# A transformer block's attention by head pairs in double PSUM banks, with rotated queries and keys transposed behind half a projection

## The chip, the cores and the metric

The kernel runs on one core of a Trainium2 chip. The metric is the device time of one execution in microseconds, as the median of several runs. The engines named below are TensorE (PE, the matmuls), VectorE (DVE), ScalarE (ACT), GpSimd (POOL) and SyncE (SP, which issues the DMAs). Each takes its instructions in the order of its own list and waits where an operand isn't ready.

## The reference

The program computes two transformer blocks in fp32, for one sequence of 256 tokens and width 1024. The change touches only the first block's mixer:

```python
h = rms_norm(x, norm1_g)
u_a, v_a, q, k, v = split(h @ w_in, ...)            # five parts of 512 columns
a_out = spatial_gating(gelu(u_a), gelu(v_a), ...)    # 8 groups, chunks of 128 tokens
q, k = apply_rope(q, cos, sin), apply_rope(k, cos, sin)   # 8 heads of 64
b_out = dilated_attention(q, k, v)                   # three banded branches, weighted by their denominators
mix = concat(rms_norm(a_out), rms_norm(b_out))
x = x + mix @ w_out
x = x + peer(rms_norm(x, norm2_g), ...)              # router and experts
```

Behind it come the experts and a second block of two hybrid layers, which the change doesn't touch.

## The kernel before, in words

Matmuls are made from two halves of each operand: a number is split into a high half (rounded by ACT, L98) and a low half (the rest, by DVE, L99), and three matmuls (`mm3`, L116 to L118) make one product. Weights come in units of 512 KB (`fetch`, L88) into a ring of four `raw` buffers; a buffer is free for the next load when its low half has been made. In the first block the units are used in this order: four for `v_a`, four each for q, k and v (`project`, matmuls of 128x512), four for the gate `u_a` (`gate_u`, matmuls of 128x256, 24 to a unit), eight for `w_out`, and then those of the router.

The order of the instructions on each engine isn't that of the source: a scheduler lays out the lists from the source's order, the dependencies and the buffers of the pools. Pools in PSUM are `ps_b` (four single banks, tag `pp`) and `ps_m` (three single banks, tag `mm`, and one for `po`). These steps matter here:

- x is transposed four blocks at a time (L234); ACT scales and rounds each (L238) and DVE makes the low half.
- `rotated` (L290 to L307) turns q or k by the rope tables: DVE multiplies and adds (L296 to L302), PE transposes the sum (L306), ACT copies it out (L307).
- `attend(hp)` makes the scores of a pair of heads (L342), each head in a bank of its own. DVE adds the mask and reduces to the maximum (L349) and negates it (L351), ACT takes the exponential and its sum (L353), DVE takes the reciprocal (L355) and scales (L357).
- `gather_v(hp)` transposes the probabilities, one head to a bank (L369), DVE copies them out (L371), and PE multiplies by v (L373) into `po`. `mixed` (L284 to L288) makes the high half, the low half and the square of the result.
- `spatial(k)` does the spatial gating's matmuls (L385) and DVE adds the bias (L387).
- `finish_half` (L274 to L281) sums squares for a norm by matmuls with a column of ones (L278); `norm_rows` (L219 to L226) normalizes a block of rows and transposes it in two halves (`transposes`, L163 to L167).

The attention and the gating are written in this order:

```python
attend(0); pps = project(2); ...
attend(1); gather_v(0); attend(2); gather_v(1); attend(3); gather_v(2); gather_v(3)
for k in range(4):
    spatial(k)
    gate_u(k)
```

Of the kernel before, what the change touches and what calls it, by code (L numbers as in the profile page):

```python
# [9 lines left out]
F32 = mybir.dt.float32  # L10
# [6 lines left out]
ALU = mybir.AluOpType  # L17
# [8 lines left out]
T = 256  # L26
# [12 lines left out]
def kernel(  # L39
# [47 lines left out]
    def load(dst, src):  # L87
        nc.sync.dma_start(out=dst, in_=src)  # L88
# [109 lines left out]
    with ExitStack() as c1:  # L198
# [4 lines left out]
        ps_b = c1.enter_context(tc.tile_pool(name="ps_b", bufs=4, space=PSUM, side="right"))  # L203
        ps_m = c1.enter_context(tc.tile_pool(name="ps_m", bufs=3, space=PSUM))

# [61 lines left out]

        def project(chunk):
            pps = [ps_b.tile([128, 512], F32, name="pp") for _ in range(2)]
            x_stationary(pps, xh, xl, [w_in_n[chunk * 4 + i] for i in range(4)])  # L270
            return pps

        def finish_half(base, name):
            ps = ps_m.tile([128, 2], F32, name="mm")  # L274
            for k in range(1, 4):
# [13 lines left out]

        def rotated(pps, dst):  # L290
            for tb in range(2):
                a = w1.tile([128, 8, 2, 32], F32, name="ra")
                b = w1.tile([128, 8, 2, 32], F32, name="rb")
                p4 = pps[tb].rearrange("p (h c j) -> p h c j", h=8, c=2)
# [7 lines left out]
                V.tensor_tensor(out=a, in0=a, in1=b, op=ALU.add)  # L302
                pt = ps_m.tile([128, 4, 128], F32, name="mm")
                af = a.rearrange("p h c j -> p (h c j)")
                for j in range(4):
                    P.transpose(out=pt[:, j, :], in_=af[:, j * 128:(j + 1) * 128], identity=id_t)  # L306
                S.activation(out=dst[:, :, tb * 128:(tb + 1) * 128], in_=pt, func=AF.Copy)  # L307
# [17 lines left out]

        pr = ps_m.tile([128, 2, 128], F32, name="mm")
        for tb in range(2):
# [9 lines left out]
        def attend(hp):  # L337
            pss = [ps_m.tile([128, 2, T], F32, name="mm") for _ in range(2)]
            for tb in range(2):
                for e in range(2):  # L340
                    s = slice(64 * e, 64 * e + 64)
                    P.matmul(out=pss[e][:, tb, :], lhsT=qT[s, hp, tb * 128:(tb + 1) * 128], rhs=kT[s, hp, :],  # L342
                             start=True, stop=True)
            for e in range(2):
                sm = w1.tile([128, 2, T], F32, name="sm", bufs=4)
                mx = w1.tile([128, 2], F32, name="mx", bufs=4)
                ls = w1.tile([128, 2], F32, name="ls", bufs=4)
                for tb in range(2):
                    V.tensor_tensor_reduce(out=sm[:, tb, :], in0=pss[e][:, tb, :], in1=mask_t[:, tb, :], scale=0.125,  # L349
                                           scalar=GONE, op0=ALU.add, op1=ALU.max, accum_out=mx[:, tb:tb + 1])  # L350
                V.tensor_scalar(out=mx, in0=mx, scalar1=-1.0, scalar2=None, op0=ALU.mult)  # L351
                for tb in range(2):
                    S.activation(out=sm[:, tb, :], in_=sm[:, tb, :], func=AF.Exp, bias=mx[:, tb:tb + 1],  # L353
                                 accum_out=ls[:, tb:tb + 1])
                V.reciprocal(out=ls, in_=ls)  # L355
                for tb in range(2):
                    V.tensor_scalar(out=sm[:, tb, :], in0=sm[:, tb, :], scalar1=ls[:, tb:tb + 1], scalar2=None,  # L357
                                    op0=ALU.mult)
                probs[2 * hp + e] = sm

        def gather_v(hp):
            po = ps_m.tile([128, T], F32, name="po", bufs=1)
            for e in range(2):
                h = 2 * hp + e
                sm = probs[h]
                pt = ps_b.tile([128, 512], F32, name="pp").rearrange("p (a b t) -> p a b t", a=2, b=2)
                for tb in range(2):
                    for sb in range(2):
                        P.transpose(out=pt[:, sb, tb, :], in_=sm[:, tb, sb * 128:(sb + 1) * 128], identity=id_t)  # L369
                pT = w1.tile([128, 2, T], F32, name="pT")  # L370
                V.tensor_copy(out=pT, in_=pt.rearrange("p a b t -> p a (b t)"))  # L371
                for sb in range(2):
                    P.matmul(out=po[64 * e:64 * e + 64, :], lhsT=vr[:, sb, h * 64:(h + 1) * 64], rhs=pT[:, sb, :],  # L373
                             start=(sb == 0), stop=(sb == 1))
            mixed(4 + hp, po)
# [4 lines left out]
        def spatial(k):  # L380
            pg = ps_m.tile([128, 2, 128], F32, name="mm")
            for e in range(2):
# [12 lines left out]
        attend(0)  # L395
        pps = project(2)
        for tb in range(2):
            S.activation(out=vr[:, tb, :], in_=pps[tb], func=AF.Copy, scale=rx[tb])
        load(ws_t, w_s)
# [647 lines left out]
```

## Time and profile before

| | before |
|---|---|
| median of 3 runs | 1279.85 us (1278.71 to 1280.3) |
| profiled execution | 1281.43 us, of which the span is 1279.3 us |
| busy in the span | PE 97%, DVE 76%, ACT 50%, POOL 1% |
| granted TensorE clock | mean 0.996 of full speed |
| v's projection ends, attention begins | 62.9 us |
| last weighted sum of the attention ends | 82.1 us |
| gate's projections end | 93.2 us |

The times of the trace count from the start of the span. Busy shares are over the whole span; the part that the change touches lies in its first 122 us. A row of a timeline gives the start and the length of an instruction, or of several in a row (x4), its engine, line and tiles, and in brackets the idle time before it with what ended it. Most matmuls of fp32 operands that aren't split show as two records.

### The profile page before, as it was taken

The numbers are of one execution on the slowest core, as the hardware profiler recorded it, in microseconds if no ns is written. First come the engines' busy times: TensorE is split into PE (matmuls) and PEld (weight loads), VectorE is DVE, ScalarE is ACT, GpSimd is POOL, SyncE is SP. The second block draws the span as 40 slices with busy tenths as digits, with TensorE's granted clock in tenths as the row PEclk, the third lists the DMA queues.
The fourth block names the chain that finished last, engine by engine and source line by source line (L and its number), as shares of the span: only waits on it lengthen the run. The fifth ranks groups of instructions, "written<-read, shape, count | busy, mean of one in ns | idle before, by whom it ended". The sixth has DMA issues, their size and how long they took to land.

```text
span 1279.3 us, 22833 instructions
## 1 busy us (share of the span) xinstructions
PE 1247.1 (97%) x8952; PEld 1108.9 (87%) x8952; DVE 975.2 (76%) x1907; ACT 641.4 (50%) x1031; POOL 14.8 (1%) x27
## 2 busy tenths in 40 slices
PE   7999999999999999999999999999999999999997
PEld 5777998999999999998888888788878998789995
DVE  6877899944466999998999997655566766768565
ACT  7556544444454443344444445544445566354661
POOL 0001000000000000000000000000000000000000
PEclk9999999999999999999999999999999999999999
DMA  7723555565555445455555556855555634355420
GB/s 258 258 82 127 165 164 167 174 199 186 182 188 169 161 163 166 165 163 184 178 172 179 180 171 235 287 194 191 188 168 176 192 125 132 110 206 191 139 83 33
DMA packets 61819, 219.10 MB, mean 171 GB/s; under 512 B 7064, under 2 KB 8496, under 8 KB 61584
## 3 DMA queue, kind: packets, MB, share of 16 engines
q1 hardware_dynamic: 60272, 213.03, 50.4%
q0 software_dynamic: 1440, 4.62, 1.2%
q8 instruction: 70, 1.15, 0.4%
q14 instruction: 37, 0.30, 0.1%
HBM read 214.33 MB, written 3.16 MB: 170 GB/s over the span
## 4 chain that ended last, share of the span: by engine, by line
PE 85%; DVE 8%; ACT 4%; DMA 2%; issue 1%; SPq 0%; DVEq 0%; ACTq 0%
PE pu L116 9%; PE pv L116 9%; PE pu L118 9%; PE pu L117 9%; PE pv L118 9%; PE pv L117 9%; PE pp L118 7%; PE pp L117 7%; PE pp L116 7%; DVE ulo L99 3%; PE pg L656 1%; PE pg L657 1%; ACT uhi L98 1%; PE mm L795 1%; PE rt_ps L116 1%
## 5 line engine op out<-in xcount | busy, mean ns | idle before, releaser
L99 DVE TENSOR_TENSOR ulo<-raw,uhi 128x1024 fp32r<-128x1024 f32 x390 | 474.9, 1221 | 164.7 <-ACT uhi L98 164.2
L98 ACT ACTIVATE uhi<-raw 128x1024 fp32r<-128x1024 f32 x390 | 411.3, 1056 | 338.4 <-PE pu L117 205.2
L116 PE MATMUL pu<-xh,uhi 128*128 128x256 f32 x1024 | 293.8, 287 | 2.2 <-ACT ga L462 2.2
L118 PE MATMUL pu<-xh,ulo 128*128 128x256 f32 x1024 | 292.5, 286 | 1.6 <-DVE ulo L99 1.5
L117 PE MATMUL pu<-xl,uhi 128*128 128x256 f32 x1024 | 290.8, 284 | 0.0
L116 PE MATMUL pv<-uhi,wh 128*128 128x512 f32 x512 | 203.9, 398 | 0.4 <-ACT wh L98 0.4
L118 PE MATMUL pv<-uhi,wl 128*128 128x512 f32 x512 | 200.9, 392 | 0.6 <-DVE wl L99 0.6
L117 PE MATMUL pv<-ulo,wh 128*128 128x512 f32 x512 | 200.5, 392 | 0.0
L116 PEld LDWEIGHTS pu<-xh,uhi 128*128 128x128 f32 x1024 | 196.8, 192 | 3.9 <-ACT ga L462 3.1
L118 PEld LDWEIGHTS pu<-xh,ulo 128*128 128x128 f32 x1024 | 196.9, 192 | 3.4 <-DVE ulo L99 2.6
L117 PEld LDWEIGHTS pu<-xl,uhi 128*128 128x128 f32 x1024 | 196.9, 192 | 0.0
L116 PE MATMUL pp<-xh,uhi 128*128 128x256 f32 x496 | 141.4, 285 | 0.0
L118 PE MATMUL pp<-xh,ulo 128*128 128x256 f32 x496 | 141.0, 284 | 0.0
L117 PE MATMUL pp<-xl,uhi 128*128 128x256 f32 x496 | 140.6, 284 | 0.0
L98 ACT ACTIVATE wh<-ga 128x256 fp32r<-128x256 f32 x128 | 53.0, 417 | 173.9 <-PE pv L117 171.9
L118 PEld LDWEIGHTS pv<-uhi,wl 128*128 128x128 f32 x512 | 96.1, 188 | 22.9 <-DVE wl L99 1.2
L116 PEld LDWEIGHTS pv<-uhi,wh 128*128 128x128 f32 x512 | 96.2, 188 | 20.6 <-ACT wh L98 0.8
L117 PEld LDWEIGHTS pv<-ulo,wh 128*128 128x128 f32 x512 | 96.3, 188 | 20.0
L118 PEld LDWEIGHTS pp<-xh,ulo 128*128 128x128 f32 x496 | 94.1, 190 | 1.1 <-issue 1.0
L116 PEld LDWEIGHTS pp<-xh,uhi 128*128 128x128 f32 x496 | 94.2, 190 | 0.9 <-issue 0.7
L117 PEld LDWEIGHTS pp<-xl,uhi 128*128 128x128 f32 x496 | 94.1, 190 | 0.6 <-issue 0.4
L659 DVE SCALAR_TENSOR_TENSOR ga<-pg,ga 128x288 f32<-128x288 f32 (+1 forms) x96 | 87.2, 939 | 7.3 <-PE pg L657 7.3
(271 smaller groups left out, 1643.9 us busy)
## 6 DMA issues: line engine op xcount, KB each, us to landing
raw<-in_expert_u_dram SPq DMA_DIRECT2D x128, 512.0 KB, 3.4
raw<-in_expert_v_dram SPq DMA_DIRECT2D x128, 512.0 KB, 3.3
raw<-in_w_t_dram SPq DMA_DIRECT2D x58, 512.0 KB, 3.6
raw<-in_w_out_dram SPq DMA_DIRECT2D x24, 512.0 KB, 3.4
raw<-in_w_in_n_dram SPq DMA_DIRECT2D x16, 512.0 KB, 5.5
raw<-in_w_n_dram SPq DMA_DIRECT2D x16, 512.0 KB, 3.3
raw<-in_w_query_dram SPq DMA_DIRECT2D x12, 512.0 KB, 3.8
raw<-in_w_in_t_dram SPq DMA_DIRECT2D x4, 512.0 KB, 4.5
```

Of the source, the lines that this page charges most:

```text
L98: S.activation(out=hi, in_=src, func=AF.Copy)
L99: eng.tensor_tensor(out=lo, in0=src, in1=hi.bitcast(F32), op=ALU.subtract)
L116: P.matmul(out=ps, lhsT=lh, rhs=rh, start=start, stop=False)
L117: P.matmul(out=ps, lhsT=lh, rhs=rl, start=False, stop=False)
L118: return P.matmul(out=ps, lhsT=ll, rhs=rh, start=False, stop=stop).ins
L656: P.matmul(out=pg[:, t - lo_t, :], lhsT=o1[:, q, :, l], rhs=oh[:, q, :, l], start=True, stop=False)
L657: P.matmul(out=pg[:, t - lo_t, :], lhsT=o1[:, q, :, l], rhs=ol[:, q, :, l], start=False, stop=True)
L659: V.scalar_tensor_tensor(out=gv, in0=pg, scalar=1.0 / 32768.0, in1=gv, op0=ALU.mult, op1=ALU.mult)
L795: P.matmul(out=po[64 * e:64 * e + 64, tb, :], lhsT=v[:, sb, h * 64:(h + 1) * 64], rhs=w[:, e, n * 128:(n + 1) * 128], start=(sb == 0), sto ...
```

## The change

It does five things.

- `ps_m` becomes two double banks (`banks(n)`, tags `mm0` and `mm1`, one buffer each); all else takes a single bank of `ps_b` (`one_bank()`). The transposes of x and those of `norm_rows` put both halves of a row block into one double bank.
- `project` works by halves of two units. q's rotated transposes stand behind the first half of k's projection, k's behind the first half of v's; the rotation works in a tile that shares its buffers with the transposed probabilities.
- `attend` puts both heads of a pair into the double bank `mm0`: four reductions, one negation, four exponentials, one reciprocal and four scalings.
- `gather_v` puts the eight transposes of a pair into the double bank `mm1`, copies them out in one instruction, and runs the sums by v with both heads side by side.
- The mask is loaded ahead of the gain `g_v`.

```diff
...
-        ps_m = c1.enter_context(tc.tile_pool(name="ps_m", bufs=3, space=PSUM))
+        ps_m = c1.enter_context(tc.tile_pool(name="ps_m", bufs=1, space=PSUM))
+        def banks(n):
+            return ps_m.tile([128, 2, 512], F32, name="mm", tag=f"mm{n % 2}")
+        def one_bank():
+            return ps_b.tile([128, 512], F32, name="pp")
...
             r = rms_scale([src[:, 0:512], src[:, 512:1024]], scr)
+            bk = banks(tb)
...
-                transposes(ps_pool, xn, xh, xl, tb, 4 * n, 4)
+                transposes(ps_pool, xn, xh, xl, tb, 4 * n, 4, bk[:, n, :])
...
         for tb in range(2):
+            bk = banks(tb)
             for q in range(0, KD, 4):
-                pt = ps_m.tile([128, 4, 128], F32, name="mm")
+                pt = bk[:, q // 4, :].rearrange("p (j t) -> p j t", j=4)
...
-        def project(chunk):
-            pps = [ps_b.tile([128, 512], F32, name="pp") for _ in range(2)]
-            x_stationary(pps, xh, xl, [w_in_n[chunk * 4 + i] for i in range(4)])
-            return pps
+        def project(chunk, pps, half):
+            x_units([(pps + [0, 6], w_in_n[chunk * 4 + c], 2 * c) for c in range(2 * half, 2 * half + 2)], xh, xl)
...
-        rotated(project(0), qT)
+        ppq, ppk = [[one_bank() for _ in range(2)] for _ in range(2)]
+        project(0, ppq, 0)
+        project(0, ppq, 1)
+        rot = rotated(ppq)
+        project(1, ppk, 0)
+        transposed(rot, qT)
+        project(1, ppk, 1)
+        load(mask_t, att_mask.rearrange("(b p) s -> p b s", p=128))
+        rot = rotated(ppk)
+        ppv = [one_bank() for _ in range(2)]
+        project(2, ppv, 0)
+        transposed(rot, kT)
         bcast(g_v.rearrange("p a b -> p (a b)"), gains[0, 1024:2048], load)
-        rotated(project(1), kT)
-        load(mask_t, att_mask.rearrange("(b p) s -> p b s", p=128))
...
         def attend(hp):
-            pss = [ps_m.tile([128, 2, T], F32, name="mm") for _ in range(2)]
+            pss = banks(0)
...
+            each = [(e, tb, slice(tb * T, (tb + 1) * T), slice(2 * e + tb, 2 * e + tb + 1))
+                    for e in range(2) for tb in range(2)]
+            for e, tb, c, n in each:
+                V.tensor_tensor_reduce(out=sm[:, e, c], in0=pss[:, e, c], in1=mask_t[:, tb, :], scale=0.125,
+                                       scalar=GONE, op0=ALU.add, op1=ALU.max, accum_out=mx[:, n])
+            V.tensor_scalar(out=mx, in0=mx, scalar1=-1.0, scalar2=None, op0=ALU.mult)
+            for e, tb, c, n in each:
+                S.activation(out=sm[:, e, c], in_=sm[:, e, c], func=AF.Exp, bias=mx[:, n], accum_out=ls[:, n])
+            V.reciprocal(out=ls, in_=ls)
...
         def gather_v(hp):
-            po = ps_m.tile([128, T], F32, name="po", bufs=1)
+            sm = probs[hp]
+            pt = banks(1)
...
+            pT = w1.tile([128, 2, 512], F32, name="pT", tag="wide")
+            V.tensor_copy(out=pT, in_=pt)
+            po = one_bank()[:, 0:T]
...
         attend(0)
-        pps = project(2)
+        project(2, ppv, 1)
...
```

**Where the instructions moved.** On PE, at q's rotation: L306 before and L318 now are the transposes of the rotated sum (`ra`, now `ab`); the matmuls around them belong to k's projection. Before, they stood behind its third matmul (and the second four behind its twelfth):

```order
L116 MATMUL pp<-uhi,xh 128x512
L117 MATMUL pp<-ulo,xh 128x512
L306 MATMUL mm<-id_t,ra 128x128 x4
L118 MATMUL pp<-uhi,xl 128x512
L116 MATMUL pp<-uhi,xh 128x512
```

Now all eight stand behind its twenty-fourth:

```order
L117 MATMUL pp<-ulo,xh 128x512
L118 MATMUL pp<-uhi,xl 128x512
L318 MATMUL pp<-id_t,ab 128x128 x8
L116 MATMUL pp<-uhi,xh 128x512
L117 MATMUL pp<-ulo,xh 128x512
```

The matmuls between are the same; 21 of them now run before the transposes.

On PE, in the attention: L342 before and L363 now are the scores, L369 and L387 the transposes of the probabilities, L373 and L395 the sums by v, L385 and L407 the spatial gating. Before:

```order
L342 MATMUL mm<-kT,qT 128x256 x3
L385 MATMUL mm<-ws_t,vn 64x128 x2
L373 MATMUL po<-pT,vr 64x256 x4
L385 MATMUL mm<-ws_t,vn 64x128
L369 MATMUL pp<-id_t,sm 128x128 x2
L385 MATMUL mm<-ws_t,vn 64x128
L369 MATMUL pp<-id_t,sm 128x128 x6
L385 MATMUL mm<-ws_t,vn 64x128 x8
L373 MATMUL po<-pT,vr 64x256 x4
L385 MATMUL mm<-ws_t,vn 64x128 x2
L369 MATMUL pp<-id_t,sm 128x128 x4
L385 MATMUL mm<-ws_t,vn 64x128 x2
```

Now:

```order
L363 MATMUL mm<-kT,qT 128x256 x3
L395 MATMUL pp<-pT,vr 64x256 x4
L363 MATMUL mm<-kT,qT 128x256
L387 MATMUL mm<-id_t,sm 128x128 x8
L363 MATMUL mm<-kT,qT 128x256 x3
L395 MATMUL pp<-pT,vr 64x256 x4
L363 MATMUL mm<-kT,qT 128x256
L387 MATMUL mm<-id_t,sm 128x128 x8
L395 MATMUL pp<-pT,vr 64x256 x4
L387 MATMUL mm<-id_t,sm 128x128 x8
L395 MATMUL pp<-pT,vr 64x256 x4
L407 MATMUL pp<-ws_t,vn 64x128 x4
```

The gating's matmuls, which before stood between the steps of the attention, now come behind its last sum, the other three steps each among the gate's matmuls; and each step of the attention works on a whole pair.

On DVE, in the attention: L349 before and L371 now are the reductions, L371 before and L390 now the copies of the transposed probabilities, L351 and L373 the negations, L355 and L376 the reciprocals, L357 and L378 the scalings, L292 the low half in `mixed`. Before, from the second pair's last reduction on:

```order
L349 ISA sm,mx<-mm,mask_t 128x256
L349 ISA mx 128x1
L371 COPY pT<-pp 128x512
L351 TENSOR_SCALAR mx<-mx 128x2
L371 COPY pT<-pp 128x512
L355 RECIPROCAL ls<-ls 128x2
L349 ISA sm,mx<-mm,mask_t 128x256
L349 ISA mx 128x1
L357 TENSOR_SCALAR sm<-sm,ls 128x256 x2
L355 RECIPROCAL ls<-ls 128x2
```

Now, from the same reduction on:

```order
L371 ISA sm,mx<-mm,mask_t 128x256
L371 ISA mx 128x1
L390 COPY pT<-mm 128x1024
L373 TENSOR_SCALAR mx<-mx 128x4
L99 TENSOR_TENSOR ulo<-raw,uhi 128x1024 x2
L376 RECIPROCAL ls<-ls 128x4
L371 ISA sm,mx<-mm,mask_t 128x256
L371 ISA mx 128x1
L378 TENSOR_SCALAR sm<-sm,ls 128x256 x4
L292 SCALAR_TENSOR_TENSOR ml<-pp,g_t,mh 128x256
```

One copy stands for two, and the negation comes behind it for the whole pair, so that no exponential of a pair can start before all its reductions and the copy of the pair before. Two weight splits (L99) stand between.

## Rows read from the trace of the kernel before

**Rows 1.** The page: busy time by engine; the chain that ended last

```profile
PE 1247.1 (97%) x8952; PEld 1108.9 (87%) x8952; DVE 975.2 (76%) x1907; ACT 641.4 (50%) x1031; POOL 14.8 (1%) x27
...
PE 85%; DVE 8%; ACT 4%; DMA 2%; issue 1%; SPq 0%; DVEq 0%; ACTq 0%
```

**Rows 2.** Waits of PE, 0 to 130 us: total, times, longest

```profile
PE mm L306 <- DVE ra L302: 1.7, 1, 1.7
```

**Rows 3.** Timeline of PE, 30 to 100 us: start, length, operation, idle before

```profile
36.24 0.39 PE L116 MATMUL pp<-uhi,xh 128*128 128x512 f32 x1
36.47 0.39 PE L117 MATMUL pp<-ulo,xh 128*128 128x512 f32 x1
38.59 0.66 PE L306 MATMUL mm<-id_t,ra 128*128 128x128 f32 x4 [1.73 <-DVE ra L302]
39.00 0.48 PE L118 MATMUL pp<-uhi,xl 128*128 128x512 f32 x1
```

**Rows 4.** Window of the attention: width; busy PE, PEld, DVE, ACT, POOL; granted clock

```profile
62.90:82.10 19.20, 18.70 (x126) 12.26 (x125) 17.02 (x64) 10.48 (x32) 1.46 (x2) 1.00 0.08 29
```

**Rows 5.** Timeline of PE, attention and end of the gate projections

```profile
71.97 1.08 PE L373 MATMUL po<-pT,vr 128*64 128x256 f32 x8
...
75.03 1.40 PE L385 MATMUL mm<-ws_t,vn 128*64 128x128 f32 x16
...
80.52 1.57 PE L373 MATMUL po<-pT,vr 128*64 128x256 f32 x8
...
93.16 0.50 PE L278 MATMUL mm<-ones,sq 128*128 128x1 f32 x4
```

**Rows 6.** Timeline of DVE, 40 to 95 us

```profile
43.71 1.22 DVE L99 TENSOR_TENSOR ulo<-raw,uhi 128x1024 fp32r<-128x1024 f32 x1
44.85 0.69 DVE L323 TENSOR_TENSOR vn<-vn,g_v 128x512 f32<-128x512 f32 x1
...
48.32 0.75 DVE L300 TENSOR_TENSOR rb<-pp,rope_t 128x256 f32<-128x256 f32 x2
...
64.13 0.42 DVE L349 CUSTOM_DVE_ANT_0 sm<-mm,mask_t 128x256 f32<-128x256 f32 x1
...
67.26 0.61 DVE L357 TENSOR_SCALAR sm<-sm,ls 128x256 f32<-128x256 f32 x2
67.79 0.16 DVE L355 RECIPROCAL ls<-ls 128x2 f32<-128x2 f32 x1
...
68.72 0.47 DVE L286 SCALAR_TENSOR_TENSOR ml<-po,g_t,mh 128x256 fp32r<-128x256 f32 x1
```

**Rows 7.** Timeline of ACT, 20 to 60 us

```profile
21.51 1.28 ACT L312 ACT_TABLE_LOAD   x1
```

**Rows 8.** The page: DMA issues, KB each, us to landing

```profile
raw<-in_w_out_dram SPq DMA_DIRECT2D x24, 512.0 KB, 3.4
...
raw<-in_w_in_t_dram SPq DMA_DIRECT2D x4, 512.0 KB, 4.5
```

**Rows 9.** The page: costliest groups: busy, mean ns of one

```profile
L98 ACT ACTIVATE uhi<-raw 128x1024 fp32r<-128x1024 f32 x390 | 411.3, 1056 | 338.4 <-PE pu L117 205.2
```

**Rows 10.** Timeline of ACT, 55 to 85 us: four exponentials, first and last

```profile
65.37 0.51 ACT L353 ACTIVATE sm<-sm,mx 128x256 f32<-128x256 f32 x1 [0.66 <-DVE mx L351]
...
66.89 0.49 ACT L353 ACTIVATE sm<-sm,mx 128x256 f32<-128x256 f32 x1
```

**Rows 11.** Groups on tile pT: ns min/median/max

```profile
L371 DVE COPY pT<-pp x8: 680/685/692, 65.6 to 80.3; 128x512 f32<-128x512 f32 x8
L883 DVE COPY pT<-mm x8: 949/950/954, 1038.1 to 1252.9; 128x768 f32<-128x768 f32 x8
```

**Rows 12.** Timeline, 112 to 131 us: the first norm's low halves

```profile
117.81 1.29 DVE L167 TENSOR_TENSOR xl<-mm,xh 128x512 fp32r<-128x512 f32 x2
```

**Rows 13.** Timeline of PE, 10.8 to 15 us

```profile
12.60 0.63 PE L116 MATMUL pp<-uhi,xh 128*128 128x512 f32 x1
13.03 0.63 PE L117 MATMUL pp<-ulo,xh 128*128 128x512 f32 x1
```

More of the change, by code (lines that the diff above doesn't have):

```diff
@@ L266 @@
         x1 = [p1.tile([128, D], F32, name=f"x1_{tb}") for tb in range(2)]
-        def project(chunk):
-            pps = [ps_b.tile([128, 512], F32, name="pp") for _ in range(2)]
-            x_stationary(pps, xh, xl, [w_in_n[chunk * 4 + i] for i in range(4)])
-            return pps
+        def project(chunk, pps, half):
+            x_units([(pps + [0, 6], w_in_n[chunk * 4 + c], 2 * c) for c in range(2 * half, 2 * half + 2)], xh, xl)
         def finish_half(base, name):
-            ps = ps_m.tile([128, 2], F32, name="mm")
+            ps = one_bank()[:, 0:2]
             for k in range(1, 4):
@@ L288, in mixed, with rotated @@
             S.activation(out=sq[:, k, :], in_=src, func=AF.Square)
-        def rotated(pps, dst):
+        def rotated(pps):
+            out = []
             for tb in range(2):
-                a = w1.tile([128, 8, 2, 32], F32, name="ra")
-                b = w1.tile([128, 8, 2, 32], F32, name="rb")
+                ab = w1.tile([128, 2, 512], F32, name="ab", tag="wide")
+                a = ab[:, 0, :].rearrange("p (h c j) -> p h c j", h=8, c=2)
+                b = ab[:, 1, :].rearrange("p (h c j) -> p h c j", h=8, c=2)
                 p4 = pps[tb].rearrange("p (h c j) -> p h c j", h=8, c=2)
@@ L302, in rotated, with transposed @@
                 V.tensor_tensor(out=a, in0=a, in1=b, op=ALU.add)
-                pt = ps_m.tile([128, 4, 128], F32, name="mm")
-                af = a.rearrange("p h c j -> p (h c j)")
+                out.append(ab[:, 0, :])
+            return out
+        def transposed(rot, dst):
+            for tb in range(2):
+                pt = one_bank().rearrange("p (j t) -> p j t", j=4)
                 for j in range(4):
-                    P.transpose(out=pt[:, j, :], in_=af[:, j * 128:(j + 1) * 128], identity=id_t)
+                    P.transpose(out=pt[:, j, :], in_=rot[tb][:, j * 128:(j + 1) * 128], identity=id_t)
                 S.activation(out=dst[:, :, tb * 128:(tb + 1) * 128], in_=pt, func=AF.Copy)
@@ L323 @@
             V.tensor_tensor(out=vn[:, tb, :], in0=vn[:, tb, :], in1=g_v[:, 1, :], op=ALU.add)
-        pr = ps_m.tile([128, 2, 128], F32, name="mm")
+        pr = one_bank()[:, 0:256].rearrange("p (b t) -> p b t", b=2)
         for tb in range(2):
@@ L341, in attend @@
                     s = slice(64 * e, 64 * e + 64)
-                    P.matmul(out=pss[e][:, tb, :], lhsT=qT[s, hp, tb * 128:(tb + 1) * 128], rhs=kT[s, hp, :],
-                             start=True, stop=True)
-            for e in range(2):
[L345 to L359, printed above, removed]
@@ L361, in gather_v @@
-        def gather_v(hp):
-            po = ps_m.tile([128, T], F32, name="po", bufs=1)
[L363 to L366, printed above, removed]
+                    P.matmul(out=pss[:, e, tb * T:(tb + 1) * T], lhsT=qT[s, hp, tb * 128:(tb + 1) * 128],
+                             rhs=kT[s, hp, :], start=True, stop=True)
+            sm = w1.tile([128, 2, 512], F32, name="sm")
@@ new lines, in attend @@
+            mx = w1.tile([128, 4], F32, name="mx")
+            ls = w1.tile([128, 4], F32, name="ls")
+            each = [(e, tb, slice(tb * T, (tb + 1) * T), slice(2 * e + tb, 2 * e + tb + 1))
[3 more added lines that the diff above has]
+                                       scalar=GONE, op0=ALU.add, op1=ALU.max, accum_out=mx[:, n])
@@ new lines, in attend, with gather_v @@
+            V.tensor_scalar(out=mx, in0=mx, scalar1=-1.0, scalar2=None, op0=ALU.mult)
+            for e, tb, c, n in each:
+                S.activation(out=sm[:, e, c], in_=sm[:, e, c], func=AF.Exp, bias=mx[:, n], accum_out=ls[:, n])
+            V.reciprocal(out=ls, in_=ls)
+            for e, tb, c, n in each:
+                V.tensor_scalar(out=sm[:, e, c], in0=sm[:, e, c], scalar1=ls[:, n], scalar2=None, op0=ALU.mult)
+            probs[hp] = sm
+        def gather_v(hp):
+            sm = probs[hp]
+            pt = banks(1)
+            for e in range(2):
@@ L367, in gather_v @@
                 for tb in range(2):
                     for sb in range(2):
[L369 to L374, printed above, removed]
+                        P.transpose(out=pt[:, e, sb * T + tb * 128:sb * T + tb * 128 + 128],
+                                    in_=sm[:, e, tb * T + sb * 128:tb * T + sb * 128 + 128], identity=id_t)
@@ L375, in gather_v @@
+            pT = w1.tile([128, 2, 512], F32, name="pT", tag="wide")
+            V.tensor_copy(out=pT, in_=pt)
+            po = one_bank()[:, 0:T]
+            for sb in range(2):
+                for e in range(2):
+                    h = 2 * hp + e
+                    P.matmul(out=po[64 * e:64 * e + 64, :], lhsT=vr[:, sb, h * 64:(h + 1) * 64],
+                             rhs=pT[:, e, sb * T:(sb + 1) * T], start=(sb == 0), stop=(sb == 1))
             mixed(4 + hp, po)
@@ L380, in spatial @@
         def spatial(k):
-            pg = ps_m.tile([128, 2, 128], F32, name="mm")
+            pg = one_bank()[:, 0:256].rearrange("p (c t) -> p c t", c=2)
             for e in range(2):
@@ L395 @@
         attend(0)
-        pps = project(2)
+        project(2, ppv, 1)
         for tb in range(2):
-            S.activation(out=vr[:, tb, :], in_=pps[tb], func=AF.Copy, scale=rx[tb])
+            S.activation(out=vr[:, tb, :], in_=ppv[tb], func=AF.Copy, scale=rx[tb])
         load(ws_t, w_s)
```

## The prediction

> **What bounds the kernel now.** I read the page first. TensorE (PE) is busy 97% of the span and carries 85% of the chain of waits that ended last; VectorE (DVE) carries 8% [rows 1]. So a microsecond counts only where PE stands idle, where its list gets longer, or where another engine sets its pace. From the router's projections behind the first norm on, the lists of all engines are the same in both programs, so the shift that the change leaves at about 122 us should reach the end unaltered.
>
> Then PE's waits over the first 130 us: inside the changed part they name 1.7 us, once, for DVE's last addition of q's rotation [rows 2]. PE's timeline shows where: after the third matmul of k's projection, at 36.47, the next thing is the transposes at 38.59 [rows 3].
>
> Then the windows: the attention (62.9 to 82.1 us) holds 18.70 us of PE in 19.20, DVE at 17.02, ACT at 10.48 [rows 4]. PE is full there because the scheduler laid the spatial gating (32 records at L385) into the gaps of the attention. PE records overlap, so busy time is not price: 16 of these records take 1.40 us [rows 5], which is 0.70 per step of eight and 2.8 us for the four steps. DVE's records overlap too: a split of 1.22 us that starts at 43.71 is followed at 44.85 [rows 6], so I price every DVE row at its length less 0.08.
>
> **The front: 1.7 us off PE, little of it at the end.** q's transposes stand 21 matmuls later; at 0.2275 us each (36.24 to 36.47) [rows 3] that is 4.8 us, and the 1.73 us wait goes. Against it: the x transposes of a block's second half wait for readers of the first, and ACT has two more table loads at 1.28 us [rows 7]. I put 0 on these, because a delay there eats only what the wait gives back; 1 us at worst.
>
> PE ends k's projection at 36.70 + 45 × 0.2275 + 0.8 (eight transposes; four take 0.41) [rows 3] = 47.7. But the attention is opened by DVE, whose list has ahead of the first negated maximum: what is left of k's rotation (a multiply and an addition of 128x512 at 0.61, two halves at 0.67, and one more 128x512 of the gating's norm at 0.61) [rows 6], to 50.2; four splits at 1.14, to 54.8; a small copy, 0.3; a fifth split. The load of that fifth unit can start when the first of the four has been read, at 51.3; it takes 4.5 us to land [rows 8] and its ACT half 1.06 [rows 9]: 56.9, so the split ends at 58.0. Four score reductions at 0.34 [rows 6] follow, to 59.4, and a sixth split, to 60.5. **The first exponential can start at 60.5**, and what PE gained at the front waits for it.
>
> **The attention: a serial chain per pair.** Before, each head had its own bank, maxima and reciprocal: the exponentials of one head ran beside reductions and copies of another. Now a pair has one double bank, one maximum tile and one reciprocal, and there is one such score buffer. DVE's list then gives, per pair: four exponentials on ACT (65.37 to 67.38, 2.05 us) [rows 10], reciprocal and negation (0.08 each), four scalings (two take 0.53, so 1.06) [rows 6], the next pair's four reductions (1.38), and a 128x1024 copy. That copy isn't in the trace: 128x512 costs 0.685 and 128x768 0.950 [rows 11], 0.265 per 256 elements, so 1.22, or 1.14 from start to start. The ends are 0.87 (the last 256 for nothing) and 1.2 (two copies of 512); I take the line, whose two points it continues.
>
> From one negated maximum to the next, by the list:
> - pair 0 to 1: exponentials 2.05 (a split lies under them), 0.08, scalings 1.06, reductions 1.38, copy and negation 1.22 = 5.8.
> - 1 to 2: two splits hide the exponentials, 2.28; 0.08; one reduction 0.34; scalings 1.06; the low half of a mixed output 0.39 [rows 6]; three reductions 1.02; 1.22 = 6.4.
> - 2 to 3: 2.05 (two reductions under it) + 0.08 + 0.34 + 1.06 + 0.39 + 0.34 + 1.22 = 5.5.
> - the tail: 2.05 + 0.08 + 1.06 + 0.39, the copy 1.14, 0.2 for the last transposes and the weighted sum 1.08 (71.97) [rows 5] = 6.0.
>
> Together 23.7, so the last weighted sum ends at **84.2**; before, at 82.1 (80.52 + 1.57) [rows 5]. **+2.1.** PE has at most 18.7 − 2.8 = 16 us of work in that time [rows 4, 5], so it is covered.
>
> With separate banks the attention cost PE only 19.20 − 18.70 = 0.5 us of idleness [rows 4]. The Trainium skill ("Perfetto Trace Analysis", section Matmuls) has independent matmul groups rotate through different PSUM banks, so that the evacuation of one overlaps the matmuls of the next. The trace of before agrees with it; the change gives the scores one buffer, and with a second the sum would be nearer to that of rival 2.
>
> **The gating behind it: +3.3.** All four spatial steps now stand among the gate's matmuls, where PE has no gap: +2.8 (2.0 if some fall beside waits, 3.2 if an evacuation shows). The gate before took 93.16 − 82.09 = 11.1 us [rows 5] for 92 of its 96 matmuls, 0.12 each; the four that stood in the attention's gaps come back: +0.5. It ends at 84.2 + 2.8 + 11.6 = 98.6 against 93.16: +5.4.
>
> **The norm: +0.5.** The second half of a row block shares a double bank with the first, so its transposes wait for DVE's reads. Two halves of that work take 1.29 us [rows 12], one 0.64; there are two such places, less what other matmuls fill: 0 to 1.3, taken 0.5. The mask's load ahead of the gain's, the single banks for the small sums, and the tile shared by rotation and probabilities I put at 0, hidden under DVE's splits, and at 0.3 each without that cover.
>
> **Sum:** 2.1 + 2.8 + 0.5 + 0.5 = +5.9 on the profiled execution's 1281.43 us, which lies 1.58 above the median. On the median, 1279.85, that is **1285.8 us**. Bounds: less 1.1 if the fifth unit lands as fast as the 3.4 us ones [rows 8], 0.4 if k ends earlier, 0.8 in the chain (DVE reductions that slip under exponentials), 0.8 in the gating: −3.1 in all. More by four hand-offs of 0.25, 1 at the front, 0.4 in the gating, 0.4 in the norm: +2.8. Its own range is 1282.7 to 1288.6. A measurement of this kernel can tell about 0.2%, 2.56 us, from no change.
>
> **Rivals.**
> 1. *PE keeps the pace (faster).* If DVE comes early everywhere, the 1.7 us of the front and fewer, larger DVE instructions (one copy for two, one reciprocal for two) reach the end. Its place is the last weighted sum; it decides if that ends before 78.3 (84.2 − 5.9), 17.8 us after 60.5 or under 4.5 per pair. For it: the wait at the transposes is certain to go. Against: exponentials and scalings alone are 3.1 of each pair, and the list puts reductions and copy behind them. The time: 1.7 less, and 1 to 2 of the attention: 1276 to 1278. Chance 0.09.
> 2. *The exponentials hide (no change).* If the next reductions slip under the exponentials, DVE's own rate decides: 1.38 + 1.14 + 0.16 + 1.06 + 0.39 = 4.1 per pair, plus two splits, 18.8 in all, to 79.3; then 2.8 + 11.6 to 93.7, +0.5, and the norm's 0.5: 1280.9. Against: each engine runs its list in order, and the list holds the reductions behind the scalings. 0.15.
> 3. *PE's clock falls (slower still).* PE has at most 16 us of work in 23.7, with gaps in each pair. Against it: the granted clock was 1.00, the upper level (2.4 GHz), through the attention before [rows 4]. For a price: the first matmuls of the run stand 0.43 apart [rows 13] against 0.2275 later. At such a pace the last transposes and weighted sum (0.2 + 1.08) cost 1.3 more, and 2 us of the gate's work, my estimate of how long it would last, 2 more: 3.3, so 1289.1. The Trainium skill ("TensorE: Matmul & The Clock Gate", section on HAM oscillation) tells of kernels whose waits bring the slower clock; no row here shows that after the start. 0.07.
> 4. *It doesn't do what it says:* the wait moves from q's transposes to k's. DVE opens the attention anyway, so this changes nothing at the end and lies within my range.
>
> **How the numbers follow.** Forecast 0.69, rivals 0.09, 0.15, 0.07. Slower by over 0.2%, above 1282.41: the forecast less 0.02 for its lowest corner, and rival 3: 0.74. Within 0.2%: rival 2 and that 0.02: 0.17. Faster: 0.09. The range, 1280.3 to 1289.3, leaves out rival 1, the lower half of rival 2 and rival 3's upper tail: about 2 in 10.
>
> **What would show it.** Right: no wait at q's transposes; the first exponential at 60.5 ± 0.8; negated maxima 5.5 to 6.4 us apart with PE idle in each pair; the last weighted sum's end at 84.2; the gate's last matmul at 98.6; the norm's second transposes waiting for DVE. Wrong: maxima under 4.5 us apart (rivals 1, 2), a granted clock below 1.00 (rival 3), or a difference at 98 us that isn't the one at the end.

## The result, and the profile after

The changed kernel takes 1294.76 us (median of 4 runs, 1294.34 to 1297.88), the kernel before, beside it, 1279.38 us: a ratio of 1.0118 with the interval 1.0105 to 1.013. That is 15.4 us slower, where 5.9 were forecast and 1289.3 us was the top of the range.

The shares of the page hardly move, so they answer nothing by themselves:

```profile
PE 1251.6 (97%) x8952; PEld 1110.6 (86%) x8952; DVE 975.1 (75%) x1895; ACT 644.0 (50%) x1033; POOL 14.4 (1%) x27
```

PE's waits from 30 to 110 us (who waits for whom, total, times, longest), against [rows 2]:

```profile
PE mm L387 <- DVE sm L378: 5.0, 4, 1.6
PE pp L395 <- DVE pT L390: 2.6, 2, 1.3
PE mm L363 <- DVE mx L371: 1.9, 2, 1.0
```

The wait for q's rotation is gone, as forecast. In its place PE waits 9.5 us inside the attention, for scaled probabilities, for copies and for score banks that DVE hasn't read yet. Those waits were in the sum. What wasn't stands in the windows of the same stretch (width; busy PE, PEld, DVE, ACT, POOL; granted clock; share of DMA; GB/s), where [rows 4] had 1.00 throughout:

```profile
60.00:65.00 5.00, 3.83 (x23) 2.44 (x21) 3.14 (x10) 5.00 (x13) 0.00 (x0) 1.00 0.84 274
65.00:70.00 5.00, 2.84 (x16) 1.54 (x16) 5.00 (x15) 2.96 (x10) 0.00 (x0) 1.00 0.14 43
70.00:75.00 5.00, 3.91 (x18) 2.53 (x20) 3.38 (x12) 1.90 (x8) 0.00 (x0) 0.69 0.51 170
75.00:80.00 5.00, 3.37 (x13) 1.78 (x10) 2.61 (x13) 1.03 (x4) 0.00 (x0) 0.50 0.00 0
```

From 60 to 70 us PE works 3.83 and 2.84 us of each 5 at a clock of 1.00; from about 72 us the clock is at half, the lower of its two levels (1.2 GHz). In windows of 1 us, the fall and the return:

```profile
71.00:72.00 1.00, 0.25 (x2) 0.01 (x1) 1.00 (x6) 0.38 (x1) 0.00 (x0) 0.94 0.78 172
72.00:73.00 1.00, 0.77 (x4) 0.69 (x5) 1.00 (x3) 0.00 (x0) 0.00 (x0) 0.50 0.72 295
...
91.00:92.00 1.00, 1.00 (x7) 0.75 (x4) 0.78 (x2) 0.38 (x1) 0.00 (x0) 0.50 0.00 0
92.00:93.00 1.00, 1.00 (x9) 1.00 (x8) 0.00 (x0) 0.00 (x0) 0.73 (x1) 0.82 0.00 0
93.00:94.00 1.00, 1.00 (x11) 1.00 (x10) 0.00 (x0) 0.00 (x0) 0.00 (x0) 1.00 0.00 0
```

It falls at about 72 us and comes back at about 92 us, when the gate's matmuls fill PE. PE's timeline shows the same forms of instruction on both sides of the fall:

```profile
65.88 1.13 PE L363 MATMUL mm<-kT,qT 64*128 64x256 f32 x6 [0.94 <-DVE mx L371]
67.10 1.08 PE L395 MATMUL pp<-pT,vr 128*64 128x256 f32 x8
...
70.11 1.14 PE L387 MATMUL mm<-id_t,sm 128*128 128x128 f32 x8 [1.30 <-DVE sm L378]
72.23 2.07 PE L363 MATMUL mm<-kT,qT 64*128 64x256 f32 x6 [0.98 <-DVE mx L371]
74.23 1.98 PE L395 MATMUL pp<-pT,vr 128*64 128x256 f32 x8
76.14 1.22 PE L363 MATMUL mm<-kT,qT 64*128 64x256 f32 x2
78.99 1.94 PE L387 MATMUL mm<-id_t,sm 128*128 128x128 f32 x8 [1.64 <-DVE sm L378]
...
88.44 1.98 PE L395 MATMUL pp<-pT,vr 128*64 128x256 f32 x8 [1.32 <-DVE pT L390]
```

Six scores take 1.13 us at 65.88 and 2.07 at 72.23; eight records of a weighted sum 1.08 at 67.10 and 1.98 at 74.23; eight transposes 1.14 and 1.94. Each of these stands on the chain of its pair, so the chain gets longer. DVE shows it ahead of the fourth pair's first reduction, where it sits idle until the pair's last score (76.14 + 1.22 = 77.36) is there:

```profile
77.39 0.42 DVE L371 CUSTOM_DVE_ANT_0 sm<-mm,mask_t 128x256 f32<-128x256 f32 x1 [4.01 <-PE mm L363]
```

DVE's negated maxima, one per pair:

```profile
59.87 0.16 DVE L373 TENSOR_SCALAR mx<-mx 128x4 f32<-128x4 f32 x1
...
66.87 0.16 DVE L373 TENSOR_SCALAR mx<-mx 128x4 f32<-128x4 f32 x1
...
73.23 0.16 DVE L373 TENSOR_SCALAR mx<-mx 128x4 f32<-128x4 f32 x1
...
82.11 0.16 DVE L373 TENSOR_SCALAR mx<-mx 128x4 f32<-128x4 f32 x1
```

They are 7.0, 6.4 and 8.9 us apart; the last weighted sum ends at 88.44 + 1.98 = 90.4. PE's first matmul of the sums of squares closes the gate, and the first transposes of the norm follow:

```profile
105.65 0.50 PE L284 MATMUL pp<-ones,sq 128*128 128x1 f32 x4
...
129.03 0.60 PE L163 MATMUL mm<-id_t,xn 128*128 128x128 f32 x4
```

Against 93.16 [rows 5] the gate ends 12.5 us later, and the norm begins 12.5 us later too (it began at 116.54).

### The profile page after: what moved, and what is told of

Read it like the earlier page. It is cut to its first block, busy times and chain, and to the rows that moved or that the text cites. A ratio compares the mean times of both kernels' runs of the same rounds, so it can differ in the third digit from the quotient of the medians.

```text
span 1292.4 us, 22827 instructions
## 1 busy us (share of the span) xinstructions
PE 1251.6 (97%) x8952; PEld 1110.6 (86%) x8952; DVE 975.1 (75%) x1895; ACT 644.0 (50%) x1033; POOL 14.4 (1%) x27
## 4 chain that ended last, share of the span: by engine, by line
PE 84%; DVE 9%; ACT 4%; DMA 2%; issue 1%; SPq 0%; DVEq 0%; ACTq 0%
PE pu L116 9%; PE pu L118 9%; PE pu L117 9%; PE pv L116 9%; PE pv L118 9%; PE pv L117 9%; PE pp L116 7%; PE pp L118 7%; PE pp L117 7%; DVE ulo L99 3%; PE pg L678 1%; PE pg L679 1%; ACT uhi L98 1%; PE mm L817 1%; DMA raw<-in_expert_v_dram 1%
## 5 line engine op out<-in xcount | busy, mean ns | idle before, releaser
L99 DVE TENSOR_TENSOR ulo<-raw,uhi 128x1024 fp32r<-128x1024 f32 x390 | 474.4, 1220 | 158.8 <-ACT uhi L98 158.3
L116 PE MATMUL pu<-xh,uhi 128*128 128x256 f32 x1024 | 293.4, 287 | 2.3 <-ACT ga L484 2.3
L116 PE MATMUL pv<-uhi,wh 128*128 128x512 f32 x512 | 203.7, 398 | 0.5 <-ACT wh L98 0.5
L116 PEld LDWEIGHTS pu<-xh,uhi 128*128 128x128 f32 x1024 | 197.0, 192 | 3.9 <-ACT ga L484 3.1
L116 PE MATMUL pp<-xh,uhi 128*128 128x256 f32 x496 | 141.8, 286 | 0.0
L116 PEld LDWEIGHTS pv<-uhi,wh 128*128 128x128 f32 x512 | 96.1, 188 | 20.6 <-ACT wh L98 0.9
L116 PEld LDWEIGHTS pp<-xh,uhi 128*128 128x128 f32 x496 | 94.3, 190 | 1.8 <-issue 0.8
```

Source lines behind the costliest of these rows:

```text
L99: eng.tensor_tensor(out=lo, in0=src, in1=hi.bitcast(F32), op=ALU.subtract)
L116: P.matmul(out=ps, lhsT=lh, rhs=rh, start=start, stop=False)
```

## The experiments

Eleven runs were made, two of them a second profile of a kernel as it is. Each is given against the kernel before, which ran beside it.

**1. Added matmuls in PE's gaps.** In the changed kernel:

```diff
+        def fill(n):
+            bk = one_bank()
+            for i in range(n):
+                P.matmul(out=bk, lhsT=xh[:, 0, 0:128], rhs=xh[:, 0:2, :].rearrange("p a b -> p (a b)"), start=True, stop=True)
...
         attend(1)
+        fill(5)
         gather_v(0)
+        fill(5)
         attend(2)
...
```

> The changed kernel with 30 added matmuls of 128x512 in the gaps of the attention (5 at a time, before and after each pair's transposes; their result is read by nobody). Theory 1, the clock: the granted clock stays at 1.00 from 62 to 95 us, the third and fourth negated maxima stand 5.5 to 6.5 us apart instead of 8.9, the gate's last matmul ends at 99 to 102 us instead of 105.65, and the time is 1288 to 1291 us, although PE does 6.8 us more work. Rival, the chain on DVE and ACT alone sets the time and the slow clock hides under it: the gate ends at 105.6 us or later, 1295 us or more. If the clock falls in spite of the added work, nothing is decided.

Measured: 1292.25 us (ratio 1.0096, 1.0077 to 1.0115). In its profile the gate ends at 100.68 us, inside theory 1's bounds and 5.0 earlier than in the changed kernel, though PE does some 6.8 us more (30 matmuls at the 0.2275 us each of [rows 3]). The third and fourth maxima stood 7.4 us apart, with most of two groups of ten added matmuls between them, not the 5.5 to 6.5 expected. The clock (same columns as above) fell only for a while:

```profile
65.00:70.00 5.00, 3.70 (x18) 2.12 (x19) 4.90 (x17) 2.55 (x9) 0.00 (x0) 0.73 0.29 105
...
75.00:80.00 5.00, 4.12 (x26) 2.96 (x22) 4.02 (x15) 2.54 (x9) 0.73 (x1) 1.00 0.00 0
```

The time came out over the bounds: the span, 1289.8 us, is only 2.6 shorter than the 1292.4 of the changed kernel. By the stages of the trace, 3 us are given back in the second block, between its first and last sum by v (218.6 us against 215.6); there the clock was 0.98 from 1120 to 1140 us and 0.94 from 1140 to 1160, where the profile of the changed kernel has 1.00. So more work for PE made this stretch faster, which the clock explains; but the time of the whole run holds other falls as well. The added matmuls also moved other instructions: all eight records of a pair's scores now stand ahead of the weighted sum, each negation from the second on ahead of the copy, and the first maximum came 1.1 us earlier (58.80). Part of the 5.0 us can be theirs, and this run doesn't separate them.

**2. The same in every gap.** Five ahead of each pair's transposes and five before the bank of the weighted sum is taken:

```diff
         def gather_v(hp):
             sm = probs[hp]
+            fill(5)
             pt = banks(1)
...
+            fill(5)
             po = one_bank()[:, 0:T]
```

> As the first run with added matmuls, but 40 of them, 5 ahead of each pair's transposes and 5 while DVE copies the transposed probabilities out, so that every gap of PE has some. The first had a clock of 0.73 from 65 to 70 us left. Theory, the clock alone made what the sum missed: granted clock 1.00 from 60 to 95 us, negated maxima 5.5 to 7 us apart with up to 1 us each from the added work, gate's end 98.5 to 101 us. Rival, part of the loss is not the clock: gate's end over 102 us with the clock at 1.00.

Measured: 1292.27 us (1.0101, 1.0084 to 1.0117), gate's end 102.31 us. The clock is 1.00 in every window of the attention, for instance:

```profile
65.00:70.00 5.00, 3.85 (x26) 2.59 (x25) 5.00 (x14) 3.46 (x10) 0.00 (x0) 1.00 0.30 109
...
75.00:80.00 5.00, 4.94 (x30) 3.29 (x30) 3.35 (x13) 2.42 (x10) 0.87 (x1) 1.00 0.00 0
```

and the maxima are 7.1, 6.6 and 6.8 us apart, with no third one at 8.9:

```profile
60.75 0.16 DVE L373 TENSOR_SCALAR mx<-mx 128x4 f32<-128x4 f32 x1
...
67.80 0.16 DVE L373 TENSOR_SCALAR mx<-mx 128x4 f32<-128x4 f32 x1
...
74.35 0.16 DVE L373 TENSOR_SCALAR mx<-mx 128x4 f32<-128x4 f32 x1
...
81.17 0.15 DVE L373 TENSOR_SCALAR mx<-mx 128x4 f32<-128x4 f32 x1
```

The gate ends 1.3 us over theory's bound and just past the rival's 102, so by what was written ahead the rival has it: part of the loss is not the clock. How large a part is open, as some 9.1 us of added matmuls (40 at 0.2275) in a chain of four pairs also cost time on it, and this run can't separate the two. With the clock held the third interval is 2.1 us shorter than in the changed kernel, in spite of 10 added matmuls in it; the scores of that pair stand four by four around the weighted sum here, so the list differs too.

**3. The gating back in the gaps.** `spatial(0)` to `spatial(3)` are written one ahead of each `gather_v`:

```diff
         attend(1)
+        spatial(0)
         gather_v(0)
...
         for k in range(4):
-            spatial(k)
             gate_u(k)
```

> The changed kernel with the four spatial steps written into the attention, one ahead of each pair's transposes, so that they stand in PE's gaps again. Theory 1: 2.8 us leave the dense gate part and the added work holds the clock, so that 6.5 us more come back: the gate ends at 96 to 98 us, 1285 to 1287 us. If the added 0.7 us per pair is too little to hold the clock: the gate ends at 102 to 103 us, 1291 to 1292 us. Rival, where the spatial steps stand doesn't matter: 1294 to 1295 us.

Measured: 1285.35 us (1.0049, 1.0032 to 1.0065), gate's end 96.75 us: theory 1, by time and by place, 8.9 us earlier than in the changed kernel, of which 2.8 to 3.1 are the gating itself. The clock was not held entirely:

```profile
75.00:80.00 5.00, 2.38 (x16) 1.59 (x16) 3.89 (x14) 2.46 (x9) 0.72 (x1) 0.85 0.32 105
80.00:85.00 5.00, 3.59 (x28) 2.53 (x24) 2.94 (x7) 0.86 (x2) 0.73 (x1) 0.81 0.00 0
```

**4. The half projections alone,** on the kernel before (its banks, attention and norm; the lines of the change for `project`, `rotated` and `transposed`, and the mask's load in its new place):

```diff
-        rotated(project(0), qT)
+        project(0, ppq, 0)
+        project(0, ppq, 1)
+        rot = rotated(ppq)
+        project(1, ppk, 0)
+        transposed(rot, qT)
...
```

> The kernel before with one part of the change: projections by halves, and the rotated transposes behind half a projection; banks, attention, gating and norm as before. Theory 1: the 1.7 us wait goes, and as PE is full from there to the end of the gate, it reaches the end: the gate ends at 91.0 to 91.8 us instead of 93.16, 1277.0 to 1278.2 us. Rival, DVE opens the attention, as forecast for the whole change: the gate ends at 92.5 to 93.2, 1279 to 1279.5 us.

Measured: 1279.53 us in 10 runs against 1279.28 in 13 (1.0002, 0.9992 to 1.0011). The gate ended at 91.50 us, as theory 1 had it, and the time didn't move, as the rival had it. Both at once put the first profile of the kernel before in doubt.

**5. The kernel before, once more.**

> The kernel before, unchanged, for a second profile. The first profiled execution took 1281.43 us, 2 us over the median of 13 runs (1279.28). Theory: the 2 us are a clock that fell in the router (0.83 from 200 to 210 us) in that execution and not in all; a profile without that fall shows 1278 to 1279.5 us, with the gate's end at 93.0 to 93.3 us as before. Rival: the first 120 us vary from run to run, and the gate's end moves by over 0.5 us.

Measured: 1279.54 us in this execution. The 2 us are neither of the two alone. The clock fell in the router here too (0.85 from 200 to 205 us, 0.81 to 210). But the wait of 1.7 us [rows 2], on which the front's gain was priced, is this in the second profile:

```profile
PE mm L306 <- DVE ra L302: 0.2, 1, 0.2
```

and the gate ends 1.0 us earlier than in the first:

```profile
92.18 0.50 PE L278 MATMUL mm<-ones,sq 128*128 128x1 f32 x4
```

So most of that wait belonged to the one execution that was profiled first. Against this second profile the half projections end the gate 0.7 us earlier, too little for the runs to tell.

**6. The changed kernel without the half projections;** q's and k's transposes take the double banks here.

```diff
-        project(0, ppq, 0)
-        project(0, ppq, 1)
-        rot = rotated(ppq)
-        project(1, ppk, 0)
-        transposed(rot, qT)
+        transposed(rotated(project(0)), qT)
...
```

> The changed kernel without the half projections: the rotated transposes stand behind the whole projection again; double banks, the attention by pairs and the norm as in the change. Theory 1, the attention alone makes the loss and DVE opens it: the clock falls again between 70 and 74 us, and the time is 1293 to 1297 us. Rival, the half projections take part in the loss: under 1290 us.

Measured: 1295.89 us (1.0132, 1.0113 to 1.0152), theory 1 by time. The clock fell earlier than I had it: 0.50 already from 64 to 66 us, after a stretch from 62 to 64 in which PE was busy 0.08 us. The loss is made by the rest of the change, with or without the half projections.

**7. The gating's bank alone,** on the kernel before:

```diff
-            pg = ps_m.tile([128, 2, 128], F32, name="mm")
+            pg = ps_b.tile([128, 512], F32, name="pp")[:, 0:256].rearrange("p (c t) -> p c t", c=2)
```

> The kernel before with one edit: the bank of the spatial steps comes from the pool of the projections, as in the change, so that the scheduler leaves these steps behind the attention. Theory 1, the displaced steps cost their 2 to 2.8 us and the attention by heads still keeps PE busy enough for the clock: the gate ends at 95.0 to 96.0 us, granted clock 1.00 throughout, 1281 to 1282.3 us. Theory 2, it is the displaced steps whose gaps let the clock fall, whatever the form of the attention: clock under 0.9 somewhere from 65 to 85 us, gate's end over 97, 1283.5 us or more.

Measured: 1282.81 us in 7 runs, 1280.85 to 1283.71 (1.0027, 1.0015 to 1.0038). That one line is enough for the scheduler to leave the gating behind all but the last steps of the attention (its first record at 76.30, the last weighted sum from 77.30 us); that a bank of `ps_b` is handed out in the order of the source would explain it, but no run shows the reason. In the profile the clock stayed at 1.00 from 60 to 110 us, even where PE was busy for half of a window:

```profile
70.00:75.00 5.00, 2.48 (x14) 1.37 (x13) 4.95 (x17) 2.90 (x11) 0.72 (x1) 1.00 0.01 2
```

The gate ended at 93.25, 1.1 us later than in the second profile of the kernel before and lower than either theory had it; the first maxima had come 2 us earlier. That profile is of the fastest of the seven runs (1280.9 us), and the median lies between the bounds of the two theories. What the others lose beyond it wasn't seen; their mean clocks, 0.995 to 0.997, are near those of the kernel before (0.996 to 0.998), where the changed kernel had 0.987 to 0.991.

**8. Two score buffers.** In the changed kernel, successive pairs alternate between the two double banks, and the transposes take two single ones:

```diff
-            pss = banks(0)
+            pss = banks(hp)
...
-            pt = banks(1)
+            pt = [one_bank() for _ in range(2)]
...
-            V.tensor_copy(out=pT, in_=pt)
+            for e in range(2):
+                V.tensor_copy(out=pT[:, e, :], in_=pt[e])
```

> The changed kernel with two score buffers: the scores of successive pairs alternate between the two double banks, and the transposed probabilities take two single banks with a copy each. Spatial steps still behind the attention. Theory 1, the one score buffer made the chain: negated maxima 4 to 5 us apart, last weighted sum at 79 to 81 us, gate's end at 93.5 to 95.5, no clock under 0.9, 1281 to 1283 us. If the clock falls all the same: gate's end at 98 us or more, 1286 us or more. Rival, the lists' order and not the buffer makes the chain: negated maxima still 5.5 us or more apart.

Measured: 1285.42 us (1.0047, 1.003 to 1.0063), gate's end 97.12. The maxima:

```profile
60.60 0.16 DVE L373 TENSOR_SCALAR mx<-mx 128x4 f32<-128x4 f32 x1
...
66.96 0.16 DVE L373 TENSOR_SCALAR mx<-mx 128x4 f32<-128x4 f32 x1
...
71.91 0.16 DVE L373 TENSOR_SCALAR mx<-mx 128x4 f32<-128x4 f32 x1
...
76.26 0.16 DVE L373 TENSOR_SCALAR mx<-mx 128x4 f32<-128x4 f32 x1
```

6.4, 5.0 and 4.4 us apart, where one buffer had 7.0, 6.4 and 8.9. The windows show PE thinly used here too, but at a full clock:

```profile
70.00:75.00 5.00, 3.41 (x20) 1.57 (x17) 4.89 (x19) 2.81 (x10) 0.00 (x0) 1.00 0.28 105
75.00:80.00 5.00, 3.36 (x21) 1.96 (x21) 4.96 (x14) 2.82 (x10) 0.72 (x1) 1.00 0.05 13
```

From the second interval on the one buffer made the chain longer, as theory 1 says; in the third, the clock has its part as well. The time missed the theory's bounds by 2.4 us, and the gate's end by 1.6: the first interval stayed at 6.4, as the rival had it, and the weighted sums still ended at 82.8.

**9. Two score buffers and the gating in the gaps,** both edits together.

> The same with the spatial steps written into the attention ahead of each pair's transposes. Theory 1: both losses of the change are gone and the 1.7 us of the front stay: the gate ends at 91.0 to 92.5 us, clock 1.00 throughout, 1277.5 to 1279.5 us with the norm's 0.6 us still lost. Rival: DVE's own rate of some 4.1 us per pair holds it back: gate's end at 93 to 95 us, 1280 to 1282 us.

Measured: 1284.49 us (1.004, 1.0026 to 1.0054), gate's end 95.74: neither. The profile has one wait of 1.9 us for a copy and a clock of 0.66 from 75 to 80 us; how much each took of what theory 1 had promised isn't separated. No variant of the pairs came down to the kernel before.

**10. The norm's transposes in single banks.**

```diff
-            bk = banks(tb)
...
-                transposes(ps_pool, xn, xh, xl, tb, 4 * n, 4, bk[:, n, :])
+                transposes(ps_pool, xn, xh, xl, tb, 4 * n, 4, one_bank())
```

> The changed kernel with the norm's transposes in single banks again, so that the second half doesn't wait for DVE's reads of the first; all else as in the change. Theory: from the norm's first transposes to the first expert matmul 58.5 us, as before (116.54 to 175.1), instead of 59.2 (129.03 to 188.2), and 0.6 us off the time, which the runs can hardly tell: 1293.5 to 1295 us. Rival, the 0.6 us comes from elsewhere: 59.1 us or more.

Measured: 1299.48 us (1.0153, 1.0136 to 1.017): a miss. With these banks the scheduler left no other matmuls between the norm's two groups of eight transposes, and PE waited 3.4 us for the second row block, whose transposes then took 1.97 us against 1.03 for the first, with the clock at 0.87 from 130 to 135 us and 0.50 to 140; from the norm to the experts the trace takes 65.5 us, not 58.5. The 0.6 us stay unproved by an edit.

**11. The changed kernel, once more.**

> The changed kernel, unchanged, for a second profile. Theory: the clock falls to 0.50 in the attention again, between 66 and 76 us, as its cause is in the program; gate's end 104 to 107 us. Rival, the fall is an accident of that execution: clock 1.00 and a gate's end at 98 to 100 us.

Measured: 1295.87 us in this execution, gate's end 106.17. The fall is the program's, its moment isn't; it came just behind 65 us here, a little ahead of the bounds, and the clock was back for a while from 75 to 80 us:

```profile
60.00:65.00 5.00, 3.32 (x22) 2.21 (x20) 2.81 (x9) 5.00 (x13) 0.00 (x0) 1.00 0.80 288
65.00:70.00 5.00, 4.07 (x16) 1.94 (x14) 4.67 (x13) 2.89 (x9) 0.00 (x0) 0.56 0.15 43
70.00:75.00 5.00, 3.94 (x16) 2.69 (x15) 3.67 (x14) 0.86 (x2) 0.00 (x0) 0.50 0.50 185
75.00:80.00 5.00, 3.37 (x19) 1.91 (x16) 2.59 (x13) 2.44 (x9) 0.00 (x0) 0.84 0.00 0
```

The maxima followed the clock:

```profile
59.83 0.16 DVE L373 TENSOR_SCALAR mx<-mx 128x4 f32<-128x4 f32 x1
...
67.16 0.16 DVE L373 TENSOR_SCALAR mx<-mx 128x4 f32<-128x4 f32 x1
...
75.29 0.16 DVE L373 TENSOR_SCALAR mx<-mx 128x4 f32<-128x4 f32 x1
...
82.57 0.16 DVE L373 TENSOR_SCALAR mx<-mx 128x4 f32<-128x4 f32 x1
```

They are 7.3, 8.1 and 7.3 us apart, where the first profile had 7.0, 6.4 and 8.9. In the first the third interval was the slow one, with the clock at 0.50; here it is the second, and the third is shorter again, with the clock at 0.84 up to 80 us. It is the same program with the same lists, and PE and DVE wait only for each other from the second maximum to the fourth, so this difference is put down to the clock; of all the runs this one shows it without another change beside it.

## Why the prediction was wrong

**The front: right in mechanism, over-priced.** The wait at q's transposes went and the opening of the attention is DVE's, as forecast: the first negated maximum started at 59.87 us. The first exponential stood at 61.00 against 60.5, because ACT's list has a copy of v's projection (`vr`, 0.67 us) ahead of it, which I had not priced:

```profile
60.43 0.67 ACT L420 ACTIVATE vr<-pp,rs_z 128x512 f32<-128x512 f32 x1
61.00 0.50 ACT L375 ACTIVATE sm<-sm,mx 128x256 f32<-128x256 f32 x1
```

The 1.7 us that were to go were an accident of one execution (experiment 5), and alone they are worth nothing that can be measured (experiment 4). Rival 4 had the same result for another reason.

**The chain: right as long as the clock held.** From the first exponential, the second and the third maximum were forecast for 66.3 and 72.7 us; they came at 66.9 and 73.2, both late by the half microsecond of the start. The copy of 128x1024 took 1.22 us, as extrapolated from [rows 11]. Experiment 8 shows what the one score buffer costs: with two, the second interval fell from 6.4 to 5.0 us at a full clock in both. The rule of the Trainium skill ("Perfetto Trace Analysis", section Matmuls) speaks against one buffer, and these traces agree with it.

**The third link and the tail: the step that failed.** "2 to 3" was to take 5.5 us and took 8.9; the tail was to take 6.0 and took 90.4 − 82.1 = 8.3. Both ran at half the clock. With 0.5 for the late start, 3.4 + 2.3 for these two and 0.8 in the gating and the gate (15.2 us from the last weighted sum to the gate's end, 14.4 forecast) that is the 7.0 us by which the gate's end missed its 98.6. Not all of it is the clock's. From its first score to its last the third pair took 2.94 us, with the weighted sum between (65.88 to 68.82); at that pace the fourth pair's last score would have ended at 75.2 and not at 77.4. These 2.2 us, 0.6 that the copy behind waits for the transposes, 0.8 and 0.9 for the last transposes and the last weighted sum, and 0.9 in the first gate unit (4.58 us from its gating step to the next, 3.65 later) make 5.4 us for the clock, an estimate from these rows. The late start and about 1.1 us of hand-offs are the rest, so the part of the sum that doesn't hang on the clock came within 1.6 us.

This was rival 3, and both its chance, 0.07, and its price, 3.3 us, were too low. The price counted only the last pieces and the first of the gate, as if the fall came at the end of the attention. It came before the third of four pairs, and then every link waits for doubled transposes, scores and sums. The chance rested on one sentence: that no row of the trace shows a wait bringing the slower clock after the start. The trace does show it, in the first block, where PE makes an expert's product (`pu`) beside the router's steps, and where I had not looked. PE waits there once:

```profile
PE pu L116 <- ACT ga L462: 2.2, 1, 2.2
```

and the windows around that wait (columns as in [rows 4]) read:

```profile
200.00:205.00 5.00, 2.75 (x18) 1.93 (x17) 5.00 (x14) 2.89 (x5) 0.00 (x0) 1.00 0.45 169
205.00:210.00 5.00, 5.00 (x31) 5.00 (x31) 5.00 (x5) 2.58 (x4) 0.00 (x0) 0.66 0.16 36
```

PE was busy 2.75 of 5 us, and in the next 5 us the clock was 0.66 with PE full. PE was to be busy for at most 16 of 23.7 us by my own sum, much thinner than anything in the attention before. With that row beside it, the fall deserved far more than 0.07, and half the clock for every piece behind it was its price. Certain it was not: the same trace has 3.27 us of PE in the window from 35 to 40 us, and experiment 7 has 2.48 from 70 to 75 us, both with a clock of 1.00 in that window and the next. The Trainium skill ("TensorE: Matmul & The Clock Gate", section on HAM oscillation) tells of kernels whose waits, for DMAs there, bring the slower clock. The trace agrees, with waits for VectorE of 1.6 us at most: 0.50 from 75 to 90 us here.

**The gating: right.** A gate unit with its spatial step takes 3.65 us (94.89 to 98.54, DVE's products), 0.77 above the 2.88 of before, where 0.70 was priced; in the gaps it costs less (experiment 3).

**The norm: right in size, not in place.** From its first transposes to the first expert matmul 59.2 us passed (129.03 to 188.2), 58.6 before (116.54 to 175.1): +0.6, forecast +0.5. But none of its transposes waits for DVE, which was to be the sign: other matmuls stand between them (131.04, 133.03 and 135.14 us begin the later ones), and the one wait that PE has behind them is for ACT, 0.7 us, 0.4 longer than the 0.3 of before. So most of the 0.6 us lies there; the rest is open.

**Carried to the end: nearly.** Span against span the loss is 1292.4 − 1279.3 = 13.1 us; the medians differ by 15.4. The first profile of the kernel before was 2 us slow, by the accidental wait and by 1 us in the experts' second half. Against its second profile the spans differ by 15.0: 13.5 at the gate's end, 0.6 in the norm, 1.1 in the experts' second half (370.7 us against 369.6, from the first to the last L116 matmul into `pv`), which isn't explained, and 0.2 less in the rest.

## What to carry to other kernels

Before work is taken out of PE's gaps, or a chain put between its matmuls, search the whole trace for the places where PE was thinly used and read the granted clock just behind them; if it falls at one of them, price the new thin stretch at half the clock for its whole length, as a case of its own with a chance to match. Thin use didn't settle it here: some thin stretches kept the full clock. A bank's pool can decide where the scheduler puts independent work: one line moved the gating out of the gaps. A single wait in a single profile needs a second profile before a change is built on it.

## What was unexpected in the hardware

- The same program lost its clock at about 72 us in one execution and near 65 us in another, and had it back in between in one of the two.
- With some 6.8 us of matmuls that nobody reads in the gaps, the stretch ended 5.0 us earlier, in part perhaps by the order that they changed.
- With two score buffers PE was busy 3.41 and 3.36 us in windows of 5, with the clock at 1.00 in both, and with the gating's bank alone 2.48 us at 1.00; why it held there and fell in the changed kernel is not shown by any run.
- One profile and the next of the same program differed by 1.0 us at the gate's end and by 1.0 us in the experts' second half (370.6 and 369.6).
